# A hybrid attention, RWKV and mixture-of-experts layer: banks read at the chunk's end, the branch for crowded experts at expert 24, the end reordered

## The chip, the core and the metric

The kernel runs on one core of a Trainium2 chip. The metric is the time of one execution on the device in microseconds; lower is better. The core has TensorE (PE in the profile; PEld is its weight load), VectorE (DVE), ScalarE (ACT), GpSimd (POOL) and SyncE (SP), each with its own instruction stream that runs in order; a q behind a name is the engine's sequencer. TensorE writes to eight PSUM banks of 512 fp32 values per partition; the other engines read them out.

## The reference, cut to what matters

The input is 256 tokens of width 1024, in fp32. With weights of the usual kind:

```python
proj = x @ w_in                                   # 1024 x 5408
sh = token_shift(proj[..., :1824], mu_shift)      # t + (prev - t) * mu
y_rwkv = rwkv7_time_mix(...)                      # a recurrence over 256 steps, 8 heads of 64
y_attn = moba_attention(heads(q), heads(k), heads(v))   # 256 tokens are one block: causal softmax with rope
mixed = sigmoid(gate_a) * (y_attn @ w_attn_br) + sigmoid(gate_r) * (y_rwkv @ w_rwkv_br)
h = layer_norm(ALPHA * x + mixed @ w_out, ln1_g, ln1_b)
# moe_ffn: 32 experts, each token goes to 4 of them
logits = h @ w_router + b_router
top_vals, top_idx = top_k(logits, 4); gates = softmax(top_vals)
hid = h[tok] @ w1[e] + b1[e]                      # 1024 x 2048 for each expert
y = clamped_swiglu(hid) @ w2[e] + b2[e]           # 1024 x 1024 for each expert
acc[tok] += y * gate
out = layer_norm(ALPHA * h + acc, ln2_g, ln2_b)
```

Each expert is computed for 64 slots (CAP). Where an expert gets more than 64 tokens, extra rounds are needed; with these inputs no expert does, and the branch round that code is taken past it.

## The kernel before, in words

**Projections.** x @ w_in is done in 20 chunks of 256 columns. To keep fp32 accuracy each factor is split into a high and a low part (ACT at L128, DVE at L129), and each product is three matmuls (`mm3`, L135 to L137). A chunk is written into one bank, as two halves (h or tt) of eight steps (kt) each; chunks alternate between banks 0 and 1. Each step is a unit: a generator yields after it, and `fill(n)` puts n units of projection between other work on TensorE, so that TensorE has something to do while VectorE and ScalarE work on the recurrence, the softmax and so on. TensorE's order is the program's order (`manual_schedule`); the other engines' orders are made by the planner, within the program's data dependencies. These count a PSUM bank as a whole: an instruction of TensorE that writes into a bank waits for an earlier-written instruction that reads it, also where the two touch different halves.

The chunks' results are read out in three ways. `proj_shift` (L215) calls `shift`: a scaled copy on ScalarE (L205) and a multiply-add on VectorE (L206). `proj_tok` (L226) calls `done`: a copy on ScalarE (L258) for v, and rope on VectorE (L271 to L276) for q and k. `proj_gate` (L237) is a sigmoid on ScalarE (L245). In all three the read of a half stands behind the half's last unit (kt == 7). At L622 to L627 the rotated q and k are transposed in four groups through banks 6 and 7, and copied out by ScalarE.

**Experts.** Weights come in pairs of tiles, 2 MB each: four pairs for w1 and two for w2, for each of 32 experts. SyncE issues their loads (L733; for the last expert's w2 in nine pieces, L726). Ten pairs of buffers form a ring: `mdone` (L741) is called behind the last product that uses a pair and gives the pair to the next load; names put into `late` take a freed pair out of the ring for another use. A load also waits until the load eight before it has landed, as the eight DMA lanes (semaphores) are used in turn. For each expert TensorE does `first(e, 0)`, `first(e, 1)` (L1044) and `second(e)` (L1027), where `second` of an expert lies beside the next expert's `first`; `rows_out` (L1016, L1017) reads the result out, and `scatter` (L1009) adds it to the sums in banks 0 to 3.

**The end.** Behind the loop over experts stands the branch: each engine loads the largest token count (L1129) and jumps past the body for crowded experts, if there is none (the profile puts the jump and the semaphore steps behind it at L1206). The body uses four pairs that are free by then. Then come the second half of the last products: `second(30)`, the last expert's w2 in two halves of columns (L1221), each followed by its read-out, its scatter and its statistics (L1227), and the second norm (L1231 to L1250), whose last operations are split between VectorE, ScalarE and GpSimd.

## Time and profile before

| | us |
|---|---|
| median of 3 runs | 1246.01 (1243.99 to 1248.87) |
| the profiled execution | 1243.01, span 1241.2 |
| TensorE busy | 1133.4 (91%) |
| VectorE busy | 387.4 (31%) |
| ScalarE busy | 285.6 (23%) |
| DMA | 441.02 MB, mean 355 GB/s |

Busy shares are means over stages with different limits, so they say little here. The slices of the page cut the span into 40 parts of 31 us; the waits list what each engine waited for, with the total, the number and the longest; the timeline shows instructions in order of time, with the idle time in front of one and what ended it in square brackets.

### The profile page before, as it was taken

To read this page: it belongs to the slowest core of one execution; us is meant where nothing else is said; L and a number is where in the kernel's file an instruction comes from. 1 tells how busy PE (TensorE), PEld (TensorE's weight loads), DVE (VectorE), ACT (ScalarE), POOL (GpSimd) and SP (SyncE) were. 2 spreads that over 40 slices of the span, in tenths; PEclk is the share of its full clock that TensorE was granted. 3 is DMA by queue.
4 is the path that set the end of the run, shared out by engine and by line. 5 is a ranking of instruction groups with operands and counts; after the bars stand their busy time and mean duration, and the time that the engine had idled before them with its cause. 6 is when DMAs were issued, how large, how long until landed. Compare 5 with 4: busy or idle time off the path is not lost.

```text
span 1241.2 us, 15213 instructions
## 1 busy us (share of the span) xinstructions
PE 1133.4 (91%) x6434; PEld 596.0 (48%) x6434; DVE 387.4 (31%) x809; ACT 285.6 (23%) x577; POOL 6.5 (1%) x16
## 2 busy tenths in 40 slices
PE   8889887799999999999998989898999999999976
PEld 6678776798444343444433333343343333334322
DVE  4778466465222221222222121211121112222113
ACT  5534325444111111111111111111111111121112
POOL 0000000000000000000000000000000000000000
PEclk9999988899899999999999999999999999999997
DMA  7335423399699999999999999999999999999992
GB/s 269 106 116 156 150 94 145 135 364 380 264 429 427 428 427 429 427 427 418 426 426 430 426 427 429 428 426 428 427 428 427 429 427 428 427 427 427 428 414 87
DMA packets 45549, 441.02 MB, mean 355 GB/s; under 512 B 13010, under 2 KB 13538, under 8 KB 17954
## 3 DMA queue, kind: packets, MB, share of 16 engines
q1 hardware_dynamic: 36002, 436.93, 84.8%
q10 hardware_dynamic: 9472, 3.05, 1.1%
q8 instruction: 52, 0.85, 0.3%
q14 instruction: 23, 0.19, 0.0%
HBM read 438.13 MB, written 1.84 MB: 354 GB/s over the span
## 4 chain that ended last, share of the span: by engine, by line
DMA 49%; PE 41%; DVE 5%; ACT 4%; issue 1%; ACTq 0%; SPq 0%; DVEq 0%
DMA both<-in_w_dram 31%; DMA q<-in_w_dram 16%; PE b L1044 13%; PE b L1027 7%; PE b L135 4%; PE b L137 3%; PE b L136 3%; PE b L914 2%; DVE q L129 1%; PE b L1040 1%; ACT q L128 1%; DMA both<-in_win_dram 1%; PE b L1009 1%; PE b L1064 1%; ACT both L654 1%
## 5 line engine op out<-in xcount | busy, mean ns | idle before, releaser
L1044 PE MATMUL b<-both,s 128*64 128x512 f32 x1280 | 289.8, 600 | 20.4 <-DMA both<-in_w_dram 20.3
L1044 PEld LDWEIGHTS b<-both,s 128*64 128x64 f32 x1280 | 87.8, 138 | 204.7 <-issue 163.2
L1044 PE MATMUL b<-q,s 128*64 128x512 f32 x752 | 171.3, 601 | 4.0 <-DMA q<-in_w_dram 3.8
L1053 DVE TENSOR_SCALAR s<-b 128x256 f32<-128x256 f32 x64 | 27.2, 425 | 440.7 <-PE b L1044 440.7
L1027 PE MATMUL b<-both,s 128*64 128x512 f32 x576 | 128.9, 595 | 3.4 <-DMA both<-in_w_dram 3.4
L135 PE MATMUL b<-q,q 128*128 128x256 f32 x320 | 99.4, 311 | 33.4 <-ACT both L245 15.3
L1027 PE MATMUL b<-q,s 128*64 128x512 f32 x416 | 96.7, 612 | 8.5 <-DMA both<-in_w2l_dram 7.4
L1044 PEld LDWEIGHTS b<-q,s 128*64 128x64 f32 x752 | 51.2, 138 | 107.8 <-issue 97.6
L1069 ACT COPY s<-b 128x256 f32<-128x256 f32 x64 | 23.7, 371 | 323.0 <-PE b L1064 241.1
L137 PE MATMUL b<-q,q 128*128 128x256 f32 x320 | 93.5, 292 | 0.8 <-DVE q L129 0.8
L136 PE MATMUL b<-q,q 128*128 128x256 f32 x320 | 93.5, 292 | 0.0
L1017 DVE TENSOR_TENSOR s<-b,s 64x512 fp32r<-64x512 f32 (+1 forms) x66 | 44.4, 673 | 129.2 <-ACT s L1016 126.8
L135 PEld LDWEIGHTS b<-q,q 128*128 128x128 f32 x320 | 64.3, 201 | 41.0 <-ACT both L245 16.7
L1016 ACT CAST s<-b 64x512 fp32r<-64x512 f32 (+1 forms) x66 | 37.5, 568 | 191.2 <-PE b L1027 178.6
L1027 PEld LDWEIGHTS b<-both,s 128*64 128x64 f32 x576 | 40.4, 137 | 79.5 <-issue 77.8
L914 PEld LDWEIGHTS b<-s,s 128*128 128x128 f32 x512 | 61.7, 200 | 13.8 <-issue 13.0
L914 PE MATMUL b<-s,s 128*128 128x128 f32 x512 | 65.0, 287 | 1.4 <-DVE rt L958 0.7
L137 PEld LDWEIGHTS b<-q,q 128*128 128x128 f32 x320 | 64.3, 201 | 1.0 <-DVE q L129 1.0
L136 PEld LDWEIGHTS b<-q,q 128*128 128x128 f32 x320 | 64.7, 202 | 0.2 <-issue 0.2
L1054 ACT ACTIVATE s<-s 128x256 f32<-128x256 f32 x64 | 27.0, 421 | 143.8 <-DVE s L1053 143.8
L1027 PEld LDWEIGHTS b<-q,s 128*64 128x64 f32 x416 | 29.6, 140 | 62.4 <-issue 59.9
L129 DVE TENSOR_TENSOR q<-both,q 128x1024 fp32r<-128x1024 f32 x44 | 52.5, 1218 | 16.9 <-ACT q L128 16.6
(294 smaller groups left out, 1078.2 us busy)
## 6 DMA issues: line engine op xcount, KB each, us to landing
both<-in_w_dram SPq DMA_DIRECT2D x116, 2048.0 KB, 39.1
q<-in_w_dram SPq DMA_DIRECT2D x73, 2048.0 KB, 39.1
both<-in_win_dram SPq DMA_DIRECT2D x19, 1024.0 KB, 5.1
both<-in_wout_dram SPq DMA_DIRECT2D x4, 1024.0 KB, 7.2
both<-in_w2l_dram SPq DMA_DIRECT2D x7, 512.0 KB, 25.9
s<-in_wbr_dram SPq DMA_DIRECT2D x2, 1024.0 KB, 6.2
both<-in_wbr_dram SPq DMA_DIRECT2D x2, 1024.0 KB, 4.9
s<-in_w_dram SPq DMA_DIRECT2D x2, 1024.0 KB, 16.0
```

Source lines behind the costliest of these rows:

```text
L129: V.tensor_tensor(hl[:, 1, c], RAW[n][:, c], hl[:, 0, c].bitcast(FT), op=OP.subtract)
L135: PE.matmul(ps, lhs[0], rhs[0], start=first, stop=False)
L136: PE.matmul(ps, lhs[0], rhs[1], start=False, stop=False)
L137: PE.matmul(ps, lhs[1], rhs[0], start=False, stop=last)
L914: PE.matmul(pg[d // 4][:, d % 4], xtok[:, tt, 128 * d:128 * d + 128], oh[:, tt], start=tt == 0 and d % 4 == 0, stop=tt == 1 and d % 4 == 3)
L1016: A.copy(hi, ps)
L1017: V.tensor_tensor(lo, ps, hi.bitcast(FT), op=OP.subtract)
L1027: PE.matmul(ps[64 * n:64 * n + 64], aTs[e % 2][:, b, hf, 64 * g_:64 * g_ + 64], w[:, hf, 512 * n:512 * n + 512], start=ft == 0, stop=ft == 7)
L1044: PE.matmul(ps[64 * g_:64 * g_ + 64], XG[:, kt, 64 * j:64 * j + 64], w[:, kt % 2, 512 * g_:512 * g_ + 512], start=False, stop=kt == 7)
L1053: V.tensor_scalar(gl, pv[:, :, 0], 7.0, None, op0=OP.min)
L1054: A.activation(sw, gl, AF.Sigmoid, scale=1.702)
L1069: A.copy(aTs[e % 2][:, b], ps[:, 2 * i:2 * i + 2])
```

## The change

1. In the three projection helpers both halves of a bank are read out behind the chunk's last unit (h + kt == 8, that is h = 1 and kt = 7); the gate's two sigmoids become one over the whole bank.
2. The transposes of q and k go through banks 6, 7, 2 and 3.
3. The register load and the branch, with their body, stand at the start of expert 24 (MORE). The body's four pairs are the first four that come free from expert 21 on; they don't go back to the ring. The body itself is the same but for one small tile's place.
4. Behind the loop, the first scatter and its statistics stand between the two halves of the last expert's second product, in place of behind its first.
5. The second norm does three of its four quarters on VectorE, each as two operations with a PSUM bank between them, and the fourth on ScalarE and GpSimd; before, the third was on ScalarE and VectorE.

```diff
@@ -219,8 +219,10 @@
             for kt in range(8):
                 mm3(ps[:, h], [HL[n][:, x, kt, 128 * h:128 * h + 128] for x in range(2)], (xh[:, kt], xl[:, kt]),
                     kt == 0, kt == 7)
-                if kt == 7:
-                    shift(dst[:, f0 + h], ps[:, h], mc + h)
+                if h + kt == 8:
+
+                    for hh in range(2):
+                        shift(dst[:, f0 + hh], ps[:, hh], mc + hh)
                 yield
 
     def proj_tok(n, b, done):
@@ -230,8 +232,9 @@
             tk = slice(128 * tt, 128 * tt + 128)
             for kt in range(8):
                 mm3(ps[:, tt], (xh[:, kt, tk], xl[:, kt, tk]), [HL[n][:, x, kt] for x in range(2)], kt == 0, kt == 7)
-                if kt == 7:
-                    done(tt, ps[:, tt])
+                if tt + kt == 8:
+                    for t2 in range(2):
+                        done(t2, ps[:, t2])
                 yield
 
     def proj_gate(n, b, dst):
@@ -241,8 +244,8 @@
             for kt in range(8):
                 mm3(ps[:, h], [HL[n][:, x, kt, 128 * h:128 * h + 128] for x in range(2)], (xh[:, kt], xl[:, kt]),
                     kt == 0, kt == 7)
-                if kt == 7:
-                    A.activation(dst[:, h], ps[:, h], AF.Sigmoid)
+                if h + kt == 8:
+                    A.activation(dst, ps, AF.Sigmoid)
                 yield
 
     def units():
@@ -620,7 +623,7 @@
     qk = G_["qk"]
     qkT = slot(20, [2, 4, T])
     for f in range(4):
-        ps = bank(6 + f % 2, (2, T))
+        ps = bank((6, 7, 2, 3)[f], (2, T))
         for w in range(2):
             for tt in range(2):
                 PE.transpose(ps[:, w, 128 * tt:128 * tt + 128], qk[:, w, tt, 128 * f:128 * f + 128], ident)
@@ -1002,6 +1005,8 @@
 
     REST = (12, 14, 16, 18, 20)
 
+    MORE = 24
+
     def scatter(p, ns=(0, 1)):
         for n in ns:
             for tt in range(2):
@@ -1078,8 +1083,105 @@
                       start=True, stop=True)
         A.copy(ln2[:, i // 2, 512 * (i % 2):512 * (i % 2) + 512], ps.rearrange("p m n -> p (m n)"))
 
+    def overflow():
+
+        most = nc.values_load(cnt_i[0:1, 0:1], min_val=0, max_val=T)
+
+        spare = [v for u in range(4) for t in (pair(LATE["more", u]),) for v in (t[:, 0], t[:, 1])]
+        w = [v.rearrange("p (k n) -> p k n", k=2) for v in spare[:4]]
+        b1t, o4 = spare[4].rearrange("p (a b n) -> p a b n", a=2, b=2), spare[5].rearrange("p (a n) -> p a n", a=4)
+        sw4, sml = spare[6].rearrange("p (a n) -> p a n", a=8), spare[7]
+        xg = sml[:, 1280:1792].rearrange("p (d s) -> p d s", d=8)
+        ohf, ysb = sml[:, 0:256].rearrange("p (t x s) -> p t x s", t=2, x=2), sml[:, 256:768]
+        aT = sml[:, 768:1280].rearrange("p (b h s) -> p b h s", b=2, h=2)
+        pb = {i: bank(i) for i in (4, 5, 6, 7)}
...
+
+        with tc.If(most > CAP):
+            rot = rt[:, 0:2, :, 0:E]
+            V.tensor_scalar(rot[:, 0], posm, -float(CAP), None, op0=OP.add)
+            V.tensor_copy(rot[:, 1], gate)
+            for b in range(1, T // CAP):
+                with tc.If(most > CAP * b):
+                    with tc.For_i(0, E, 1) as e:
+                        more(e, rot)
+        return spare
+
     for e in range(E):
         p, j = divmod(e, 2)
+        if e == MORE - 3:
+            late.update({("more", u): 1 for u in range(4)})
+        if e == MORE:
+            order.__exit__(None, None, None)
+            spare = overflow()
+            order = tc.manual_schedule(engines={mybir.EngineType.PE})
+            order.__enter__()
         quarter = divmod(REST.index(e), 2) if e in REST[:4] else None
         if quarter:
             residual(*quarter)
@@ -1124,107 +1226,33 @@
         if E - 5 <= e < E - 1:
             second_norm_rows(e - E + 5)
     A.activation(lst[:, 0, 15:16], sw[:, 0:1], AF.Sqrt)
+    second(E - 2, lambda: turn(E - 1, (1,)))
+
+    def last_rows(n, fts):
+        for ft in fts:
+            b, g_, hf = ft // 4, (ft // 2) % 2, ft % 2
+            for a in range(2):
+                PE.matmul(py_[n][a][64 * a:64 * a + 64, 0:256], aTs[1][:, b, hf, 64 * g_:64 * g_ + 64],
+                          MW[E - 1, 8 + 2 * n + ft // 4][:, ft % 4, 256 * a:256 * a + 256], start=ft == 0, stop=ft == 7)
+
+    def last_out(n):
+        for a in range(2):
+            rows_out(E - 1, 512 * n + 256 * a, py_[n][a][64 * a:64 * a + 64, 0:256])
+
+    def last_scatter(n):
+        scatter(E // 2 - 1, (n,))
+        for tt in range(2):
+            V.bn_stats(out=lst[:, tt, 6 * n:6 * n + 6], in_=acc[2 * tt + n])
+
+    py_ = [[bank(4 + 2 * n + a) for a in range(2)] for n in range(2)]
+    last_rows(0, range(8))
+    last_out(0)
+    last_rows(1, range(4))
+    last_scatter(0)
+    last_rows(1, range(4, 8))
+    last_out(1)
+    last_scatter(1)
     order.__exit__(None, None, None)
-
-    most = nc.values_load(cnt_i[0:1, 0:1], min_val=0, max_val=T)
-
...
-    with tc.If(most > CAP):
-        rot = rt[:, 0:2, :, 0:E]
-        V.tensor_scalar(rot[:, 0], posm, -float(CAP), None, op0=OP.add)
-        V.tensor_copy(rot[:, 1], gate)
-        for b in range(1, T // CAP):
-            with tc.If(most > CAP * b):
-                with tc.For_i(0, E, 1) as e:
-                    more(e, rot)
-    with tc.manual_schedule(engines={mybir.EngineType.PE}):
-        second(E - 2, lambda: turn(E - 1, (1,)))
-        for n in range(2):
-            ps = [bank(4 + 2 * n + a) for a in range(2)]
-            for ft in range(8):
-                b, g_, hf = ft // 4, (ft // 2) % 2, ft % 2
-                for a in range(2):
-                    PE.matmul(ps[a][64 * a:64 * a + 64, 0:256], aTs[1][:, b, hf, 64 * g_:64 * g_ + 64],
-                              MW[E - 1, 8 + 2 * n + ft // 4][:, ft % 4, 256 * a:256 * a + 256], start=ft == 0, stop=ft == 7)
-            for a in range(2):
-                rows_out(E - 1, 512 * n + 256 * a, ps[a][64 * a:64 * a + 64, 0:256])
-            scatter(E // 2 - 1, (n,))
-            for tt in range(2):
-                V.bn_stats(out=lst[:, tt, 6 * n:6 * n + 6], in_=acc[2 * tt + n])
 
     zs = spare[0].rearrange("p (t n) -> p t n", t=2)
     ov = out_d[0].rearrange("(t p) n -> p t n", p=128)
@@ -1236,18 +1264,28 @@
         A.activation(st[:, 14:15], st[:, 13:14], AF.Sqrt, bias=eps[:, 1:2])
         V.reciprocal(st[:, 14:15], st[:, 14:15])
     A.activation(st[:, 15:16], st[:, 15:16], AF.Copy, scale=st[:, 14:15])
-    for tt in range(2):
-        zt, st = zs[:, tt], lst[:, tt]
-        for n in (1, 0) if tt else (0, 1):
-            c = slice(512 * n, 512 * n + 512)
-            if tt:
-                A.activation(zt[:, c], acc[2 * tt + n], AF.Identity, scale=st[:, 14:15], bias=st[:, 15:16])
-                for x, op in enumerate((OP.mult, OP.add)):
-                    (G if n else V).tensor_tensor(zt[:, c], zt[:, c], ln2[:, x, c], op=op)
-            else:
-                V.scalar_tensor_tensor(zt[:, c], acc[2 * tt + n], st[:, 12:13], ln2[:, 0, c], op0=OP.subtract, op1=OP.mult)
-                V.scalar_tensor_tensor(zt[:, c], zt[:, c], st[:, 14:15], ln2[:, 1, c], op0=OP.mult, op1=OP.add)
-            (nc.scalar if n and tt else nc.sync).dma_start(ov[:, tt, c], zt[:, c])
+    zp = {(0, 0): bank(4), (0, 1): bank(5), (1, 0): bank(6)}
+
+    def centred(tt, n):
+        V.scalar_tensor_tensor(zp[tt, n], acc[2 * tt + n], lst[:, tt, 12:13], ln2[:, 0, 512 * n:512 * n + 512],
+                               op0=OP.subtract, op1=OP.mult)
+
+    def scaled(tt, n):
+        c = slice(512 * n, 512 * n + 512)
+        V.scalar_tensor_tensor(zs[:, tt, c], zp[tt, n], lst[:, tt, 14:15], ln2[:, 1, c], op0=OP.mult, op1=OP.add)
+        nc.sync.dma_start(ov[:, tt, c], zs[:, tt, c])
+
+    c = slice(512, 1024)
+    A.activation(zs[:, 1, c], acc[3], AF.Identity, scale=st[:, 14:15], bias=st[:, 15:16])
+    for x, op in enumerate((OP.mult, OP.add)):
+        G.tensor_tensor(zs[:, 1, c], zs[:, 1, c], ln2[:, x, c], op=op)
+    nc.scalar.dma_start(ov[:, 1, c], zs[:, 1, c])
+    centred(0, 0)
+    centred(0, 1)
+    scaled(0, 0)
+    scaled(0, 1)
+    centred(1, 0)
+    scaled(1, 0)
 
 
 _ORDER = [(512, 1024), (0, 512), (1024, 1536), (1824, 5408)]
```

## Rows read from the trace of the kernel before

**Rows 1.** The page's slices: GB/s that the DMA engines moved, in 40 slices.
```profile
GB/s 269 106 116 156 150 94 145 135 364 380 264 429 427 428 427 429 427 427 418 426 426 430 426 427 429 428 426 428 427 428 427 429 427 428 427 427 427 428 414 87
```
**Rows 2.** Stages: length, busy PE, PEld, DVE, ACT, POOL, PE clock, DMA share, GB/s.
```profile
220.00:240.00 20.00, 13.90 (x87) 13.00 (x87) 8.95 (x12) 10.00 (x24) 0.00 (x0) 0.80 0.36 142
900.00:1200.00 300.00, 279.18 (x1402) 112.42 (x1400) 58.91 (x137) 45.86 (x111) 0.00 (x0) 0.99 1.01 427
```
**Rows 3.** TensorE's waits, 0 to 325 us: total, times, longest.
```profile
PE b L135 <- ACT both L245: 15.3, 7, 6.1
PE b L135 <- DVE both L274: 7.8, 4, 3.2
PE b L135 <- DVE both L206: 5.4, 3, 2.2
PE b L135 <- DVE s L206: 3.6, 2, 2.5
PE b L577 <- DVE both L571: 2.8, 1, 2.8
...
PE b L626 <- ACT both L627: 1.1, 1, 1.1
...
PE b L465 <- DVE s L206: 0.9, 1, 0.9
```
**Rows 4.** The timeline of TensorE: start, duration, instruction, idle time before it.
```profile
118.46 0.38 PE L135 MATMUL b<-q,q 128*128 128x256 f32 x1 [0.47 <-ACT both L245]
124.94 0.38 PE L135 MATMUL b<-q,q 128*128 128x256 f32 x1 [0.47 <-ACT both L245]
...
217.05 0.58 PE L135 MATMUL b<-q,q 128*128 128x256 f32 x1 [6.09 <-ACT both L245]
...
233.92 0.58 PE L135 MATMUL b<-q,q 128*128 128x256 f32 x1 [6.10 <-ACT both L245]
```
**Rows 5.** The timeline of ScalarE, before the first of the two long waits ends.
```profile
215.32 1.28 ACT L245 ACT_TABLE_LOAD   x1
```
**Rows 6.** Line L1206 by engine: duration in ns (min/median/max), first and last start.
```profile
L1206 SPq EVENT_SEMAPHORE  x8: 17/17/17, 1217.7 to 1218.8; - x8
...
L1206 PEldq COMPARE_BRANCH  x1: 6226/6226/6226, 1197.7 to 1197.7; - x1
...
L1206 DVEq COMPARE_BRANCH  x1: 76/76/76, 1202.7 to 1202.7; - x1
...
L1206 DVEq EVENT_SEMAPHORE  x1: 21/21/21, 1208.3 to 1208.3; - x1
```
**Rows 7.** The page's DMA issues: times, KB each, us to landing.
```profile
both<-in_w_dram SPq DMA_DIRECT2D x116, 2048.0 KB, 39.1
...
out_dram<-both SPq DMA_DIRECT2D x3, 256.0 KB, 2.0
```
**Rows 8.** The chain that ended last, 1130 us on: start, length, what.
```profile
1162.76 40.83 DMA q<-in_w_dram
```
**Rows 9.** The timeline of TensorE behind 1200 us.
```profile
1208.43 6.57 PE L1027 MATMUL b<-q,s 128*64 128x512 f32 x16 [7.38 <-DMA both<-in_w2l_dram]
...
1218.78 3.62 PE L1221 MATMUL b<-both,s 128*64 128x256 f32 x32
...
1224.65 3.67 PE L1221 MATMUL b<-both,s 128*64 128x256 f32 x32
1229.16 1.48 PE L1009 MATMUL b<-s,OT 128*128 128x512 f32 x4 [0.84 <-ACT s L1016]
```
**Rows 10.** The timeline of VectorE and GpSimd in the second norm.
```profile
1232.65 0.75 DVE L1249 SCALAR_TENSOR_TENSOR both<-both,lst,both 128x512 f32<-128x512 f32 x1
...
1233.95 2.93 POOL L1246 TENSOR_TENSOR both<-both,both 128x512 f32<-128x512 f32 x2 [1154.70 <-ACT both L1244]
...
1234.09 1.67 DVE L1249 SCALAR_TENSOR_TENSOR both<-both,lst,both 128x512 f32<-128x512 f32 x1
1235.68 2.47 DVE L1246 TENSOR_TENSOR both<-both,both 128x512 f32<-128x512 f32 x2
```

135 lines of the change are left out of this document (64 added, 71 removed).

## The prediction, made before the changed kernel ran

> **What bounds the kernel now.** I read the page's slices first, then the stage table, TensorE's waits, and the last 45 us instruction by instruction. The slices show two regimes: up to the ninth slice the DMA rate goes up and down, and from the twelfth on it stands at 414 to 430 GB/s without a break until the last but one [rows 1]. The stage table says the same of 900 to 1200 us: 427 GB/s, DMA share 1.01, TensorE busy 279.18 of 300 us [rows 2]. So the experts are bound by their weights (one load is 2.097 MB, at 427 GB/s 4.91 us; an expert has six, 29.5 us), and TensorE has 20.8 us in 10.2 experts to spare, 2.0 us each. The part before, some 320 us with TensorE busy most of the time, sets when that stream can run; the part behind the last landing is a chain. A microsecond saved in front moves the whole stream, because each weight load is released by work in front that frees its buffer. A microsecond saved on TensorE inside the stream is worth nothing.
>
> **In front: the waits in the middle of a chunk.** TensorE's waits before 325 us put 15.3 + 7.8 + 5.4 + 3.6 = 32.1 us on one instruction, L135, the first product of a unit, released by L245 (the sigmoid), L274 (the rotation) and L206 (the shift) [rows 3]. All three are readers of a projection's bank. That the waits stand in the middle of a chunk is seen in their spacing: two of them are 124.94 - 118.46 = 6.48 us apart, the length of one chunk of 48 products and its wait [rows 4]: there is one per chunk, and both rows are first products of the chunk's ninth unit. So the second half's first product waits until the first half has been read out of the same bank. The change emits both reads behind the last product. The next user of that bank is two chunks on (banks 0 and 1 alternate), so each read has a whole chunk, some 6.5 us, to finish in. The 32.1 us go as they stand; what counts is what is late next.
>
> - L245, 15.3 us in seven waits: two of them take 6.09 and 6.10 us [rows 4]. There ScalarE sits in the softmax exponentials and has to load a table (1.28 us) before the sigmoid [rows 5]. The next that needs ScalarE's result is the transpose of the scores some 30 units on; at 6.48 / 16 = 0.4 us a unit that is 12 us, and ScalarE's backlog is at most the 6 us that are waited for now. I keep 14 of 15.3; the sigmoid of chunk 18 may still hold up chunk 20 for 1 to 2.
> - L274, 7.8 us in four: these are VectorE behind its queue. The longest (3.2) stands where the recurrence has not begun, and goes. The others lie in the recurrence, where VectorE is also in the chain: L577 already waits 2.8 us for L571 [rows 3], and two rotations at once, 1.3 us each, stand in that queue. I keep 5.5.
> - L206, 9.0 us in five: consumers follow soon. The transposes of v at L465 already wait 0.9 us for a shift [rows 3]; two shifts at the end cost about 0.4 us more on each of ScalarE and VectorE at each of five such places. I keep 7.
> - Four banks in place of two for the transposes of q and k: L626 waits 1.1 us for L627's copy [rows 3]; 1.0 goes.
> - The clock: behind the two 6 us waits the same product takes 0.58 us where it takes 0.38 after a short one [rows 4], and the granted clock of 220 to 240 us is 0.80 [rows 2], so it had fallen to its lower level (1.2 of 2.4 GHz) after TensorE stood still. Without these waits I estimate 2.5 us back.
> - One 512-wide sigmoid in place of two 256-wide ones is ScalarE time that nobody waits for: 0.
>
> Sum in front: 14 + 5.5 + 7 + 1 + 2.5 = 30 us. The bounds: 32.1 + 1.1 + 3.5 = 37 above; below, all waits that VectorE released come back at the consumers (16.8 lost), both later reads cost 0.8 us at five places (4), and the clock gives nothing, which leaves about 12. I take 30, as most rows name a backlog that has a chunk's time to drain.
>
> **The branch at expert 24.** The rows of L1206 show what skipping the branch costs each engine [rows 6]. TensorE's branch instruction takes 6226 ns; VectorE's own takes 76 ns, but its next one comes 5.5 us later (1202.7 to 1208.3). SyncE then has eight semaphore steps, the last at 1218.8: it raises the count of each of the eight DMA lanes, and each only after that lane's last transfer. No engine waits for all others, but SyncE can issue nothing until every load before the branch has landed.
>
> Moved to expert 24, this empties the load queue once. Up to the branch SyncE has issued all six pairs of expert 24's stretch, since four of the ten pairs are held back from expert 21 for the branch's body. The last of the six is issued when TensorE ends second(22), about 5 pairs or 25 us before it lands. During these 25 us the DMA engines work; then they stand until SyncE's next issue comes through. A 256 KB store lands 2.0 us after its issue [rows 7], of which 0.6 is transfer at 427 GB/s, so with the issue (0.33) and the lane steps some 2 us are lost, and up to 4 when the 16 engines don't end together. I take 3; below there is no gain, above 8 if the instruction that follows has to be fetched first.
>
> TensorE loses more, but not on the path. Its stall here is that of the end now, 7.38 us, and behind it 16 products take 6.57 us where 32 of half the width take 3.62 [rows 9], so 2.9 us of lower clock: some 10 to 12 us. The stream falls back by 3 at the same place, so 7 to 9 us have to be caught up at 2.0 an expert: done by expert 28 or 29 of 31. This works only if the loads are still released in time. With six pairs a load is needed 6 x 4.91 = 29 us after the one before it in its buffer; using it up takes 3.6 [rows 9], the lag 12, the issue 1.7, other products in between up to 8: it holds with 4 us to spare. The loads' 39.1 us from issue to landing [rows 7], eight times 4.9, are only the queue's depth, and nothing is lost when it becomes 20. SyncE's own branch and register load lie inside the drain.
>
> **The end.** The last loads of the stream land at 1203.6 (first half of expert 30's second product [rows 8]), 1208.5 and, 4 MB later, at about 1218.3; SyncE's lane steps end there too [rows 6]. Now TensorE stands at the branch until 1208.43, then runs at the lower clock [rows 9]. Without it: first half 1203.6 to 1207.25; second 1208.5 to 1212.15; last product's first half 3.62, to 1215.8; half of its second half, 1.8, to 1217.6 (its piece has landed); the first scatter, which now needs no wait as the 0.84 us read-out [rows 9] lies beside those products, to 1218.8; the rest, 1.8, to 1220.6. The same point is now 1224.65 + 3.67 = 1228.3. Gain 7.7; if the clock falls in the 2.9 us pause before 1203.6, 1.8 less.
>
> The second norm: VectorE now ends 1235.68 + 2.47 = 1238.15, and one of its scalings takes 1.67 us beside GpSimd where the same one before took 0.75 [rows 10]. New are six operations, all through PSUM; the first scaling starts at 1232.65 now, and with it five of 0.75 us are left at most, so VectorE is done at about 1236.4. Then GpSimd's 2.93 us are the last, to 1236.9, in place of 1238.15; both are followed by a store of 2.0 us [rows 7]. About 1.1 us gained. By the Trainium skill, SBUF — State Buffer, section Who interferes with whom, a VectorE instruction with two SBUF inputs contends with a GpSimd one that reads SBUF, and one with at most one does not; by that rule the new scalings, with one input in PSUM, take 0.75. Were the slow one slow for another reason, two of them would take 1.67 and the 1.1 us would be gone. The trace agrees as far as it goes: 1.67 is 0.75 and the rest of GpSimd's first operation. The end together: 7.7 + 1.1, about 9 us (5.5 to 10).
>
> **Sum.** 1243.0 (the profiled execution, span 1241.2) - 30 - 9 + 3 = 1207. The median of the runs shown, 1246.0, is 3.0 above that execution, so I expect a median of 1210.
>
> **Rivals.**
> - *The waits only move.* VectorE and ScalarE are in the chains in front; half of the 30 comes back at L379, L465, L577 and the transposes. For it: VectorE releases 16.8 of the 32.1 us [rows 3]. Against it: ScalarE's 15.3 have slack behind them. 1210 + 15 = 1225.
> - *No gain in front.* The second half goes on waiting, or the wait goes to the next chunk's start because both reads end late: only the end and the branch count, 1246 - 9 + 3 = 1240. Against it: the banks alternate, and a read of less than 1 us has a chunk of 6 us to end in.
> - *Slower: the small ring starves the stream.* Place: experts 24 to 31, six pairs. If TensorE's lag passes some 16 us, a load is issued only when the queue is empty, and each of 48 pairs costs its 1.7 us of issue again: 82 us, 1246 - 39 + 82 = 1289. It decides from the 4 us above. By the Trainium skill, Runtime: NRT & Kernel Launch, section Instruction fetch mechanics, a taken branch out of the prefetched pages stalls for a fetch; that rule speaks for a stall at expert 24 on each engine, and the rows of L1206 show it on two. The lag is worked out from those rows and stays below the point; and SyncE's drain gives TensorE 25 us of landed weights.
>
> **How the numbers follow.** Forecast 0.72, waits move 0.18, no gain in front 0.05, ring starves 0.03, others 0.02. The forecast's own range is 1202 to 1222 (front 24 to 36, end 5.5 to 10, branch 2 to 6); the waits-move case reaches to 1231. So 1200 to 1231 holds 8 in 10. Half a per cent (6 us) is what can be told from no change: faster 0.94, same 0.03, slower 0.03.
>
> **What would show it.** Right: L135 no longer waits for L245, L274 or L206; the first expert product comes some 30 us earlier; the DMA rate has one dip of 2 to 4 us after expert 24's loads and TensorE one pause of 7 to 10 us about 25 us before it; TensorE waits for landings again before expert 30; no pause of TensorE over 3 us at the end. Wrong: a new wait of several us at L379, L465, L577 or L664; gaps in the DMA rate in experts 25 to 31; the stream's last landing earlier by much less than 27 us.

## The result: 1202 us in place of 1247, and the profile after

| | before | after |
|---|---|---|
| median, us | 1247.4 (1244.0 to 1249.2, 4 runs) | 1202.2 (1197.9 to 1203.5, 4 runs) |
| ratio, 95% interval | | 0.963 [0.960, 0.967] |
| span of the profiled execution, us | 1241.2 | 1200.3 |
| first bias product of expert 0 (L1040, now L1045), at us | 317.0 | 282.4 |
| the same of expert 24 | 975.1 | 948.7 |
| the same of expert 31 | 1184.3 | 1154.2 |
| from expert 0's first product to the end, us | 924.2 | 917.9 |

The forecast was 1210, the range 1200 to 1231. Read by place: 34.6 us were gained ahead of the experts. TensorE's lead (how much earlier it starts the same product than in the kernel before) is 34.8 us at expert 23, 26.4 at expert 24 and 30.1 from expert 27 on, 4.7 less than ahead of the branch. It ends at 40.9, so 10.8 come behind expert 31's first product.

The slices of the page after (GB/s, 40 of 30 us) answer to [rows 1]: saturation begins in the eleventh slice, and the branch shows as one slice at 344.

```profile
GB/s 278 127 137 135 152 206 137 324 382 279 428 428 427 428 427 428 427 426 422 426 428 428 428 428 428 428 427 428 427 428 428 420 344 428 427 427 428 428 428 239
```

TensorE's waits after, 0 to 290 us, answer to [rows 3] (L558, L580, L426, L468 and L382 were L555, L577, L423, L465 and L379). Every wait of L135 for a reader of its bank is gone (what is left at L135 is a wait for its input, L128); three waits of 2 to 3.4 us in the recurrence lead now.

```profile
PE b L558 <- DVE both L552: 3.4, 1, 3.4
PE b L580 <- DVE both L574: 3.1, 1, 3.1
PE b L426 <- DVE s L410: 2.2, 1, 2.2
PE b L468 <- DVE s L206: 1.6, 1, 1.6
...
PE b L135 <- ACT q L128: 0.9, 1, 0.9
```

The stage ahead of expert 0, TensorE alone: length, busy time (products), granted clock, DMA share, GB/s; of the kernel before, and then after.

```profile
0.00:316.99 316.99, 271.69 (x2089) 0.93 0.55 194
```
```profile
0.00:282.37 282.37, 262.30 (x2088) 0.95 0.60 218
```

Length less busy time is standing still: 45.3 before, 20.1 after, so 25.2 us of waits went. The other 9.4 are the same products in less busy time, at a higher clock (0.95 for 0.93). The clock accounts for most of them: 0.07 of 317 us is 22 us of full clock not granted, 0.05 of 282 is 14.

Line L1166 after, by engine, answers to [rows 6].

```profile
L1166 SPq EVENT_SEMAPHORE  x8: 17/17/17, 946.4 to 966.3; - x8
...
L1166 PEldq COMPARE_BRANCH  x1: 5912/5912/5912, 936.3 to 936.3; - x1
...
L1166 DVEq COMPARE_BRANCH  x1: 76/76/76, 942.8 to 942.8; - x1
L1166 DVEq EVENT_SEMAPHORE  x1: 21/21/21, 948.6 to 948.6; - x1
```

The rate while SyncE takes those steps (windows, columns as above):

```profile
958.00:960.00 2.00, 2.00 (x12) 1.00 0.87 369
960.00:962.00 2.00, 2.00 (x12) 1.00 0.71 303
962.00:964.00 2.00, 2.00 (x12) 1.00 0.53 221
964.00:966.00 2.00, 2.00 (x12) 1.00 0.08 33
966.00:968.00 2.00, 2.00 (x24) 1.00 0.42 82
968.00:970.00 2.00, 2.00 (x11) 1.00 0.68 229
```

Against 427 GB/s the six fall short by 58, 124, 206, 394, 345 and 198; times 2 us and over 427, that is 6.2 us of transfer not done. The busy share falls step by step over 8 us, from 0.98 at 956 to 0.08. It is a mean over 16 engines, so I read the steps as one engine after the other having nothing left; these views don't show the engines singly. TensorE's pause is in this trace too, and its last products (timeline) answer to [rows 9]: no pause above 0.91 us is left.

```profile
948.74 1.19 PE L1045 MATMUL b<-b1r,pick 128*128 128x512 f32 x2 [8.20 <-DVEq L1166]
...
1171.80 3.65 PE L1032 MATMUL b<-q,s 128*64 128x512 f32 x16 [0.87 <-DMA q<-in_w_dram]
...
1176.72 3.65 PE L1032 MATMUL b<-both,s 128*64 128x512 f32 x16 [0.91 <-DMA both<-in_w_dram]
1180.21 5.35 PE L1235 MATMUL b<-both,s 128*64 128x256 f32 x48
...
1189.39 1.48 PE L1014 MATMUL b<-s,OT 128*128 128x512 f32 x4 [0.84 <-ACT s L1021]
```

The second norm on VectorE, and its GpSimd part, answer to [rows 10]. Of the two scalings in the first row, the first is nearly over when GpSimd starts at 1194.18; the second runs beside it, and so do the last two operations on VectorE. Each takes 0.74 to 0.75 us.

```profile
1193.52 1.40 DVE L1275 SCALAR_TENSOR_TENSOR both<-b,lst,both 128x512 f32<-128x512 f32 x2
...
1195.63 0.75 DVE L1275 SCALAR_TENSOR_TENSOR both<-b,lst,both 128x512 f32<-128x512 f32 x1
```
```profile
1194.18 2.61 POOL L1281 TENSOR_TENSOR both<-both,both 128x512 f32<-128x512 f32 x2 [1119.62 <-ACT both L1279]
```

### The profile page after: what moved, and what is told of

It is laid out like the page before. It is cut to its first block, busy times and chain, and to the rows that moved or that the text cites. A ratio compares the mean times of both kernels' runs of the same rounds, so it can differ in the third digit from the quotient of the medians.

```text
span 1200.3 us, 15200 instructions
## 1 busy us (share of the span) xinstructions
PE 1124.0 (94%) x6434; PEld 590.3 (49%) x6434; DVE 384.2 (32%) x809; ACT 280.1 (23%) x566; POOL 6.1 (1%) x16
## 5 line engine op out<-in xcount | busy, mean ns | idle before, releaser
L1049 PE MATMUL b<-both,s 128*64 128x512 f32 x1456 | 331.9, 605 | 17.5 <-DMA both<-in_w_dram 17.4
L1049 PEld LDWEIGHTS b<-both,s 128*64 128x64 f32 x1456 | 100.8, 139 | 227.8 <-issue 190.7
L1032 PE MATMUL b<-both,s 128*64 128x512 f32 x624 | 139.7, 595 | 4.0 <-DMA both<-in_w_dram 3.2
L1049 PE MATMUL b<-q,s 128*64 128x512 f32 x576 | 132.4, 606 | 1.6 <-DMA q<-in_w_dram 1.5
L135 PE MATMUL b<-q,q 128*128 128x256 f32 x320 | 96.6, 302 | 0.9 <-ACT q L128 0.9
L137 PE MATMUL b<-q,q 128*128 128x256 f32 x320 | 92.9, 290 | 0.8 <-DVE q L129 0.8
L136 PE MATMUL b<-q,q 128*128 128x256 f32 x320 | 92.8, 290 | 0.0
L1032 PEld LDWEIGHTS b<-both,s 128*64 128x64 f32 x624 | 43.8, 137 | 86.5 <-issue 82.7
L1032 PE MATMUL b<-q,s 128*64 128x512 f32 x368 | 83.0, 597 | 0.9 <-DMA q<-in_w_dram 0.9
L1021 ACT CAST s<-b 64x512 fp32r<-64x512 f32 (+1 forms) x66 | 37.4, 567 | 189.5 <-PE b L1032 177.8
L1049 PEld LDWEIGHTS b<-q,s 128*64 128x64 f32 x576 | 39.7, 139 | 81.6 <-issue 76.7
L135 PEld LDWEIGHTS b<-q,q 128*128 128x128 f32 x320 | 63.6, 199 | 5.2 <-issue 2.6
L129 DVE TENSOR_TENSOR q<-both,q 128x1024 fp32r<-128x1024 f32 x44 | 52.4, 1218 | 10.6 <-ACT q L128 10.6
L1045 PE MATMUL b<-b1r,pick 128*128 128x512 f32 x128 | 47.2, 451 | 8.2 <-DVEq L1166 8.2
```

Source lines behind the costliest of these rows:

```text
L129: V.tensor_tensor(hl[:, 1, c], RAW[n][:, c], hl[:, 0, c].bitcast(FT), op=OP.subtract)
L135: PE.matmul(ps, lhs[0], rhs[0], start=first, stop=False)
L136: PE.matmul(ps, lhs[0], rhs[1], start=False, stop=False)
L137: PE.matmul(ps, lhs[1], rhs[0], start=False, stop=last)
L1021: A.copy(hi, ps)
L1032: PE.matmul(ps[64 * n:64 * n + 64], aTs[e % 2][:, b, hf, 64 * g_:64 * g_ + 64], w[:, hf, 512 * n:512 * n + 512], start=ft == 0, stop=ft == 7)
```

## Experiments

All ratios are to the kernel before, run beside them on the same chip. "Front" is where expert 0's first product starts in the profiled execution, "rest" the span from there to the end. Rest repeats within 2 us for the same code (922.3 to 924.3 in the five profiles with end and branch as before, 917.9 and 917.3 in the changed kernel's two); front only within about 5 (see the last group).

| run | median, us | ratio, interval | front | rest |
|---|---|---|---|---|
| gate_only | 1215.1 | 0.974 [0.971, 0.978] | 294.5 | 922.9 |
| tok_shift | 1230.3 | 0.987 [0.984, 0.990] | 307.3 | 922.3 |
| front_all | 1207.6 | 0.969 [0.966, 0.973] | 278.0 | 924.1 |
| keep_warm | 1241.1 | 0.996 [0.995, 0.998] | 312.1 | 924.3 |
| branch_end | 1204.5 | 0.966 [0.963, 0.970] | 281.2 | 920.7 |
| no_branch | 1195.7 | 0.961 [0.959, 0.963] | 278.6 | 915.3 |
| short_body | 1196.8 | 0.961 [0.959, 0.963] | 282.2 | 914.6 |
| act_loads | 1200.5 | 0.964 [0.962, 0.966] | 279.7 | 917.2 |
| old_end | 1205.2 | 0.967 [0.966, 0.969] | 283.1 | 920.1 |
| after_again | 1199.9 | 0.963 [0.961, 0.966] | 278.6 | 917.3 |
| pool_body | 1196.6 | 0.960 [0.957, 0.962] | 282.0 | 914.7 |
| warm_route | 1196.1 | 0.960 [0.957, 0.963] | 275.8 | 915.0 |

### The front, edit by edit

gate_only, on the kernel before:

```diff
-                if kt == 7:
-                    A.activation(dst[:, h], ps[:, h], AF.Sigmoid)
+                if h + kt == 8:
+                    A.activation(dst, ps, AF.Sigmoid)
```

tok_shift has the late read in `proj_shift` and `proj_tok` instead; front_all has all three late reads and the four banks.

> The kernel before with one edit: the gate's sigmoid reads its bank once, behind the chunk's last unit. My theory: ScalarE's backlog has a chunk's time to drain, so 14 of the 15.3 us that L135 waited for L245 go, and the clock gives 2.5 us back: 16 to 17 us shorter, ratio about 0.987, the first expert product 16 us earlier than before, and no wait of L135 for L245. Rival (the waits only move): half of it comes back at the next consumer of ScalarE's results, 7 to 8 us shorter, ratio about 0.994, with new TensorE waits for ScalarE of 7 us in sum.

> The kernel before with two edits: the token shift (L206) and the rotation and the copy of v (L274, L258) read both halves behind the chunk's last unit; the gate as before. My theory: 7 of 9.0 us at L206 and 5.5 of 7.8 us at L274 go: 12.5 us shorter, ratio 0.990. Rival (the waits only move, because VectorE is itself in the recurrence's chain): the 16.8 us come back at the consumers, 0 to 4 us shorter, ratio 0.997 to 1.000, and the waits for L245 stay 15 us or grow. If the edits add up, gate and these two together give the 34.6 us that the first expert product came earlier in the changed kernel; if one hides the other's gain, the sum of the two runs differs from 34.6 by more than 4.

> The kernel before with all edits in front (late reads of all three kinds, four banks for the transposes of q and k); branch and end as before. My theory: the first expert product comes 34.6 us earlier, as in the changed kernel, and the end comes 34 to 35 us earlier too, because the weight stream moves as a whole: ratio 0.972. Rival (the stream is bound by the DMA from the beginning of the kernel, and the gain in front is given back while the buffers are filled): the first expert product is early but the last landing is not, 20 us or less at the end, ratio 0.984 or more.

Measured: 30, 15 and 37 us shorter by the medians. The stages ahead of expert 0 (columns as above), gate_only, tok_shift, front_all:

```profile
0.00:294.52 294.52, 265.39 (x2088) 0.95 0.57 209
```
```profile
0.00:307.34 307.34, 270.36 (x2088) 0.93 0.56 200
```
```profile
0.00:278.00 278.00, 257.62 (x2088) 0.97 0.60 216
```

Standing still is 29.1, 37.0 and 20.4 us, so 16.2, 8.3 and 24.9 less than the 45.3 of before. The first two add up to the third (24.5): the waits are independent of each other, and gate's 16 confirm that ScalarE's backlog had a chunk's time to drain. (The late read and the merging of two sigmoids into one weren't tried apart.) The two longest waits of tok_shift that are no sigmoid show what VectorE's later reads gave back, the same as in the changed kernel:

```profile
PE b L557 <- DVE both L551: 3.4, 1, 3.4
PE b L579 <- DVE both L573: 3.1, 1, 3.1
```

So "the waits only move" is right for about half of VectorE's 16.8 us, and wrong for ScalarE's 15.3. Busy time is 6.3, 1.3 and 14.1 us less, and the clock says why. Full clock not granted in front, (1 - granted clock) x length, is 22 us before and 15, 22 and 8 in the three: gate_only gets 7 us back, tok_shift none, front_all 14. In gate_only the clock is 1.00 from 200 to 240 us, where the two long waits were. front_all has this too, and in the 20 us round the end of its front the clock stays at 1.00, where it is 0.73 and 0.76 in gate_only (280 to 300 us) and 0.84 and 0.65 in tok_shift (290 to 310). No edit touches that last stretch; the last group shows that it differs between executions.

By the medians the gate alone is worth nearly twice my 16 to 17, and gate and the rest together (44.5) are more than front_all's 37.4; by the fronts the two give 32.1, beside 34.6 in the changed kernel and 39.0 in front_all. With intervals of some 4 us on each of the three, and one profile of each, the runs don't settle whether that difference is real. The profiled execution of gate_only was the longest of its four and that of front_all the shortest, which is why their spans and medians disagree. The rival for front_all is out: the lead of 39.0 at expert 0 is 39.2 at expert 31.

### The clock by itself

keep_warm, on the kernel before (no result of these products is read):

```diff
+                if n in (18, 19) and h and not kt:
+                    dm = bank(5, (2, T))
+                    for _ in range(44):
+                        PE.matmul(dm[:, 0], HL[n][:, 0, 0, 128:256], xh[:, 0], start=True, stop=True)
```

> The kernel before with one addition: 44 products whose result nobody reads stand ahead of TensorE's two waits of 6.1 us for the sigmoid (44 x 0.12 us = 5.3 us, so the wait is filled and not shortened). My theory: the two waits cost more than their length, since TensorE runs at the lower clock for some 3.5 us behind each; with TensorE kept busy, the clock of 210 to 240 us stays at 1.0 and the first expert product comes 3 us earlier than in the kernel before (16 products of 0.21 us become 0.12 us, twice). Rival (the clock has nothing to do with these waits): the clock falls as before and the first expert product comes no earlier, or later by what the products exceed the wait.

Measured: 4.9 us shorter by the medians, though 44 products were added twice and both waits end as late as ScalarE lets them. The windows of 220 to 240 us and the first products behind the two waits, to be read against [rows 2, 4]:

```profile
220.00:240.00 20.00, 19.16 (x152) 1.00 0.41 158
```
```profile
218.53 0.38 PE L135 MATMUL b<-q,q 128*128 128x256 f32 x1 [0.82 <-ACT both L249]
...
233.65 0.39 PE L135 MATMUL b<-q,q 128*128 128x256 f32 x1 [0.84 <-ACT both L249]
```

The clock is 1.00 where it was 0.80, the product takes 0.38 us where it took 0.58. Followed product by product, keep_warm is 1.5 us late ahead of the two waits (its 1380th product starts at 196.0, before at 194.6) and 2.2 early behind them (the 1580th at 236.3 and 238.5): 3.7 us of clock from these two waits alone. The rest of the lead of 4.9 at expert 0 comes later, in the routing phase (the choice of experts and the gathering of their tokens), which this edit doesn't touch.

### The branch: at the end, gone, and with a short body

branch_end, on the changed kernel, with the hooks in the loop removed (no pair is withheld) and the body's four pairs taken from the free list:

```diff
+    order.__exit__(None, None, None)
+    spare = overflow()
+    order = tc.manual_schedule(engines={mybir.EngineType.PE})
+    order.__enter__()
     second(E - 2, lambda: turn(E - 1, (1,)))
```

no_branch removes the call of `overflow` at expert 24, and four pairs are withheld as before; short_body keeps the branch:

```diff
-            for b in range(1, T // CAP):
-                with tc.If(most > CAP * b):
-                    with tc.For_i(0, E, 1) as e:
-                        more(e, rot)
+            PE.transpose(pb[7][:, 0:128], xtok[:, 0, 0:128], ident)
+            A.copy(sml[:, 0:128], pb[7][:, 0:128])
```

> The changed kernel with the branch and its body put back behind the loop over experts (ahead of the last two second products), with the ring of ten pairs kept whole; front, order of the last products and second norm as changed. My theory: the drain at expert 24 goes (4.7 us of the stream are kept) and the stall of TensorE at the end comes back (7.4 us, and 2.9 us of lower clock behind it, of which some 2.5 us are saved by the new order of the last products): 4 to 7 us longer than the changed kernel, 1206 to 1209 by the profile, ratio to the kernel before 0.967 to 0.970. Rival (the gain at the end is the order's and the norm's alone, the branch's place is worth nothing): 4 to 5 us shorter than the changed kernel, 1196 or less, ratio 0.960. Second rival (a small ring costs the stream something too): the last landing comes more than 4.7 us earlier than in the changed kernel.

> The changed kernel without the register load, the branch and the body for crowded experts (that part is left out); the four pairs are withheld from expert 21 all the same, so the ring has six. My theory: all of the 4.7 us that the stream lost at expert 24 is SyncE's drain, and a ring of six pairs costs nothing: 4 to 5 us shorter than the changed kernel, no dip of the DMA rate after expert 24's loads, first expert products of 24 to 31 all 34 to 35 us earlier than in the kernel before. Rival (the smaller ring costs part of it): some of the 4.7 us stays, gaps in the DMA rate in experts 24 to 31 without a branch.

> The changed kernel with the branch kept at expert 24 but a body of five short instructions with no transfer in it (the rounds for crowded experts are left out). My theory: SyncE has no lane counts to raise, so it doesn't wait for the landings: the drain goes, 4 to 5 us shorter than the changed kernel. TensorE's pause of 8.2 us and the 5.7 us until VectorE's next instruction stay if they are the price of any taken branch at this place, and shrink to below 2 us if they come from the distance of the jump (the code behind it is then within what was loaded already). The time is the same either way, as that pause is off the path. Rival: SyncE's wait belongs to the branch and not to the body's transfers: same time as the changed kernel, dip of the DMA rate as there.

branch_end: TensorE's stall is back, with the lower clock behind it:

```profile
1173.01 5.08 PE L1032 MATMUL b<-q,s 128*64 128x512 f32 x16 [7.75 <-DVEq L1166]
```

Its rest is 2.8 to 3.4 us longer than the changed kernel's, a little below the 4 to 7 that I expected; by the times alone, 0.966 [0.963, 0.970] beside 0.963, the two can't be told apart. no_branch and short_body agree on the drain: at expert 31 TensorE has gained 4.7 and 4.5 us (no_branch's lead over the changed kernel grows from 3.8 to 8.5), in the rest 2.0 to 3.3. The landings in the traces, counted from expert 0's first product, show where the 6.2 us go. The loads behind the branch land 3.1 to 3.5 us later in the changed kernel's two profiles than in no_branch, and soon 4.2 to 4.7, so that is what the stream loses. The last two whole pairs (the last expert's w2 follows them in pieces) land only 2.7 to 3.3 later, since in no_branch and short_body the second last comes 6.2 us behind the one before it, where 4.9 are usual. Why it is late there stays open. The table cuts the rest at the last whole pair's landing, which is counted from expert 0's first product:

| | last whole pair lands, us | from there to the end of the last scatter | from there to the end of the span |
|---|---|---|---|
| before | 891.4 | 22.3 | 10.6 |
| after | 894.3 | 14.2 | 9.4 |
| after_again (below) | 893.8 | 14.2 | 9.4 |
| branch_end | 890.8 | 20.5 | 9.4 |
| no_branch | 891.0 | 14.9 | 9.3 |
| short_body | 891.0 | 14.2 | 9.4 |
| pool_body (below) | 891.0 | 14.2 | 9.5 |
| old_end (below) | 894.2 | 15.4 | 10.6 |

So the branch costs 6.3 us at the end (20.5 for 14.2), and the drain at expert 24 costs 2.7 to 3.3 there. In no_branch and short_body TensorE waits 2.2 us for expert 30's second product, where it waits 0.87 in the changed kernel; in no_branch its clock falls there, and the 16 products behind take 5.35 us for 3.65, which gives 0.7 back. The rate is 428 GB/s from 900 to 1150 us in no_branch, with six pairs:

```profile
900.00:1150.00 250.00, 229.67 (x1148) 0.99 1.01 428
```

So a ring of six pairs costs nothing. And short_body says what TensorE's pause is (TensorE reaches the branch there 11 us later, as the order of its work changed). Its line L1166, by engine:

```profile
L1166 PEldq COMPARE_BRANCH  x1: 236/236/236, 947.3 to 947.3; - x1
...
L1166 DVEq COMPARE_BRANCH  x1: 76/76/76, 951.7 to 951.7; - x1
L1166 DVEq EVENT_SEMAPHORE  x1: 21/21/21, 952.0 to 952.0; - x1
```

TensorE's jump takes 236 ns where it took 5912, VectorE's next instruction comes 0.3 us after its jump where it took 5.8, and there is no row for steps of SyncE at all. In these runs the pause comes with a long body, the drain with transfers in the body. By the Trainium skill, Runtime: NRT & Kernel Launch, section Instruction fetch mechanics, a taken branch whose target lies outside the code already fetched waits for a fetch; these two runs agree with it, 236 ns beside 5912, though no row shows the fetch itself.

### Who issues across the drain

act_loads: the first four loads behind the branch come from ScalarE.

```diff
+            q = nc.scalar if handover else nc.sync
...
-            nc.sync.dma_start(t.rearrange("p a b -> p (a b)"), src)
+            q.dma_start(t.rearrange("p a b -> p (a b)"), src)
```

> The changed kernel with the first four weight loads behind the branch issued by ScalarE in place of SyncE. ScalarE passes the branch in 0.5 us and does not wait for landings, and TensorE frees these pairs at about 955, 958, 962 and 966 us, before SyncE's drain ends at 966.3. My theory: the DMA engines have work through the drain, the dip of the DMA rate goes, and the end comes 3 to 4.7 us earlier than in the changed kernel, ratio to the kernel before 0.960. Rival (a load that ScalarE issues also waits for the lane's earlier load, or holds up ScalarE's sigmoids, so TensorE is late): the same time as the changed kernel or up to 5 us longer.

My theory fell. The timeline of ScalarE shows the first of these loads at 963.29, right when SyncE's last step (963.2) raises the count of the lane that the load uses, and a copy of ScalarE's own held up behind it; TensorE then waits for that copy for 3.9 us:

```profile
963.29 0.85 ACTq L739 DMA_DIRECT2D both<-in_w_dram  x2
964.18 0.37 ACT L1077 COPY s<-b 128x256 f32<-128x256 f32 x1 [16.70 <-SPq L1169]
```

The lanes are shared: a load that ScalarE issues, too, waits until the skipped body's share of its lane's count has been raised, and SyncE raises them one after the other (in the changed kernel at 951.64, 956.54, 961.42 and 966.28, each behind that lane's landing; the first load uses the lane that is raised last). So I moved the transfers in the body to other lanes. pool_body, on the changed kernel:

```diff
-                    nc.sync.dma_start(w[i], src.rearrange("o p (k n) -> p (o k) n", n=1024))
+                    nc.gpsimd.dma_start(w[i], src.rearrange("o p (k n) -> p (o k) n", n=1024))
...
-                nc.scalar.dma_start(b1t[64 * g_:64 * g_ + 64, 0, b],
+                nc.gpsimd.dma_start(b1t[64 * g_:64 * g_ + 64, 0, b],
```

> The changed kernel with the same branch at expert 24, but the transfers in its body (weights and bias rows for crowded experts) are issued by GpSimd in place of SyncE and ScalarE. My theory: what SyncE waits for behind the jump are the counts of the lanes that its own transfers in the body would have raised; with none of them there, SyncE issues on, the dip of the DMA rate goes, and the end comes 3 us earlier than in the changed kernel (as in the kernel without the body's transfers), ratio to the kernel before 0.960 to 0.962. TensorE's pause of 8 us stays, as the jump is as long as before, and costs nothing. Rival: the loads behind the branch wait for GpSimd's lanes as they waited when ScalarE issued them, no gain; second rival: the pause of 8 us then becomes what counts, 4 to 8 us longer.

Line L1166 by engine, and the 12 us in which the rate had fallen, in two windows:

```profile
L1166 POOLq EVENT_SEMAPHORE  x4: 17/43/43, 286.4 to 286.7; - x4
...
L1166 PEldq COMPARE_BRANCH  x1: 6072/6072/6072, 935.8 to 935.8; - x1
L1166 SPq COMPARE_BRANCH  x1: 50/50/50, 940.6 to 940.6; - x1
```
```profile
958.00:964.00 6.00, 6.00 (x30) 1.00 1.02 429
964.00:970.00 6.00, 6.00 (x42) 1.00 1.00 426
```

SyncE has no steps left; GpSimd passed the branch at 287 us, as it had nothing else to do. TensorE's pause stays (8.2 us) and its lag is made up by expert 27. The rest is 2.6 to 3.2 us shorter, and the last whole pair lands 2.7 to 3.3 earlier. Run side by side, the medians are 1196.6 and 1199.9; the intervals, [0.957, 0.962] and [0.961, 0.966], just overlap, so the rate and the landings carry the claim, not the times alone. This is the whole computation. No run takes the branch, so what the body costs when GpSimd issues its transfers isn't shown.

### The end's two parts

old_end puts the first scatter and its statistics back behind the first half of the last products, and restores the old second norm:

```diff
-    last_rows(0, range(8))
-    last_out(0)
-    last_rows(1, range(4))
-    last_scatter(0)
-    last_rows(1, range(4, 8))
-    last_out(1)
-    last_scatter(1)
+    for n in range(2):
+        last_rows(n, range(8))
+        last_out(n)
+        last_scatter(n)
```

> The changed kernel with the old order of the last products (first scatter and statistics behind the first half, then the second half) and the old second norm; branch at expert 24 and front as changed. My theory: the order is worth the read-out that TensorE waits for (0.84 us twice, one of them saved) and the half of the products that had to wait for the scatter, about 1.5 us together, and the norm 1.1: 2 to 3 us longer than the changed kernel. Rival (the 10.8 us at the end are mostly order and norm, not the branch's stall): 5 us longer or more. Second rival (the norm's new operations gain nothing, as VectorE's scalings are slow beside GpSimd): 1.5 us longer or less.

The rest is 2.2 to 2.8 us longer. From the end of the last scatter to the end of the span it is 1203.2 - 1192.7 = 10.5 us, with the new norm 1200.3 - 1190.9 = 9.4: the norm is worth the predicted 1.1. The order is worth 1.1 to 1.7 by the rest, 1.2 by the table above (15.4 for 14.2). In old_end VectorE's scaling beside GpSimd takes 1.67 us again, and the two operations behind it, which the new norm no longer has, 2.47:

```profile
1196.12 1.67 DVE L1274 SCALAR_TENSOR_TENSOR both<-both,lst,both 128x512 f32<-128x512 f32 x1
1197.71 2.47 DVE L1271 TENSOR_TENSOR both<-both,both 128x512 f32<-128x512 f32 x2
```

### Why the front differs between executions

after_again is the changed kernel unaltered. warm_route is pool_body with nine products on TensorE that nobody reads, in the four short waits of the routing phase:

```diff
+    def busy(n):
+        for _ in range(n):
+            PE.transpose(bz[:, 0], cA[:, 0:128], ident)
...
+        if n >= len(todo):
+            busy(2)
...
+    busy(2)
     gather_rows(pg, 0)
...
+    busy(3)
     gather_rows(pg, 1)
```

> The changed kernel once more, beside the three others of this call, as what they are compared with: 1198 to 1204 us. My theory on the spread between executions: the clock falls in the routing phase just ahead of the experts (270 to 285 us) in some executions and not in others, behind the same waits of 0.5 to 0.75 us, and moves the first expert product by 4 us (278 or 282 us).

> As the run with GpSimd's transfers, and in addition nine products on TensorE whose result nobody reads, 2 or 3 of them in each of the four waits of 0.5 to 0.75 us in the routing phase. My theory: the clock falls there because TensorE stands still for short times, so with less of it the first expert product comes at 278 us in every execution: 2 to 4 us shorter than the run without them by the median, and the executions lie closer together. Rival (the fall has another cause than these waits): the same time, or 1 us longer for the products.

Nine profiles share the changed front as it is; it is 278.0 to 283.1 us long in them. In the timeline the same 16 products of the gather, behind the same wait, take 3.78 us in the changed kernel's first profile and 2.05 in front_all's:

```profile
273.36 3.78 PE L917 MATMUL b<-s,s 128*128 128x128 f32 x16 [0.61 <-DVE rt L876]
```
```profile
272.68 2.05 PE L916 MATMUL b<-s,s 128*128 128x128 f32 x16 [0.61 <-DVE rt L875]
```

The windows of 270 to 280 us (columns as above), in the changed kernel and in front_all:

```profile
270.00:280.00 10.00, 8.04 (x39) 0.59 1.03 437
```
```profile
270.00:280.00 10.00, 8.12 (x60) 1.00 1.04 441
```

They show the granted clock at 0.57 to 0.66 in seven of the nine, and at 1.00 in front_all, no_branch and, with the added products, warm_route. From the gather's first product to expert 0's it is 5.3 us in these three, and 7.4 to 9.2 in the seven.

So the fall costs 2 to 4 us, but my theory that it alone decides between 278 and 282 fell in its own run: after_again has the fall (0.66, 8.1 us) and a front of 278.6, as its gather starts at 270.5, where the others' starts at 271.6 to 274.8. What sorts the nine is the clock of the whole front: 0.97 in the two shortest (278.0 and 278.6), 0.96 in the next two (278.6 and 279.7), 0.95 in the five of 281.2 to 283.1. The same products take 257.6 and 257.7 us of busy time at 0.97 and 261.6 to 263.9 at 0.95. Why the clock of the same code differs between executions stays open.

In warm_route the front is the earliest of all (275.8, clock 0.98), but its median is that of pool_body (1196.1 and 1196.6, ratios 0.9599 and 0.9597): the prediction of 2 to 4 us is not borne out by the times. The added products don't hold the clock up in every execution: over the whole run it is 0.980 and 0.981 in the two shortest of the five (1192.5 and 1193.0 us), but 0.973 and 0.974 in the other three (1196.1 to 1200.0), no more than pool_body's 0.971 to 0.977. Where it fell in those three isn't shown.

## Why the prediction was right, and where its terms were off

- **What bounds it.** Right. A lead in front moves the whole stream: 39.0 us at expert 0 are 39.2 at expert 31 in front_all, and its rest of 924.1 us is that of before. The rest, where end and branch were to give -9 + 3 = -6, fell by 6.3 and 6.9 us in the changed kernel's two profiles.
- **Front, the waits.** Predicted 14 + 5.5 + 7 + 1 = 27.5 us; 25.2 in the profile, near enough. The gate gave 16.2, its own 15.3 and a little behind them, the shift and the rotation 8.3 in place of 12.5: here the cover was thinner than I took it, as VectorE is in the recurrence's chain. Of the four wrong signs that I named, the waits at L577 and L465 (now L580 and L468) are there, 3.1 and 1.6 us, though only 0.3 and 0.7 longer than before; the larger new ones are at L558 and L426, which I hadn't named.
- **Front, the clock.** The mis-sized term: 2.5 us predicted, 3.5 as its upper bound. The two long waits alone cost 3.7 (keep_warm), and the same products took 9.4 us less busy time in the changed kernel, 14.1 in front_all. I priced only the products right behind two waits, and left out the other stretches of low clock; the front came out 34 to 39 us shorter in place of 30, and front_all's 39.0 is past the 37 that I had as the most.
- **The branch.** Place and mechanism right: one pause of TensorE of 8.2 us (7 to 10 predicted), then a dip of the rate, 18 us after the pause begins (some 25 predicted), TensorE's lag caught up (by expert 26, sooner than 28 or 29), and no starving afterwards. The size was too small: 6.2 us of transfer, 4.2 to 4.7 by the landings, where I took 3 and 4 at most unless a fetch came on top. I had counted the restart, and too little for the engines' unequal ends. That the last whole pair then lands 2.9 us later than before (894.3 and 891.4), my 3, is luck: 1.4 of the 4.7 come back at the last two pairs, for no reason that I had named.
- **The end.** 7.7 + 1.1 predicted. By the table, the last scatter ends 14.2 us behind the last whole pair where it was 22.3, so 8.1, and the norm gave 1.1; with the 2.9 this makes the 6.3 by which the rest fell. The norm's 1.1 is in part luck: its last operation ends 1.6 us sooner behind the last scatter (5.9 for 7.5), more than my 1238.15 - 1236.9 = 1.25, and the store behind it, ScalarE's now, gives some of that back. By the Trainium skill, SBUF — State Buffer, section Who interferes with whom, a VectorE instruction with at most one input in SBUF does not contend with GpSimd, outside its 2-port modes; the trace is in keep with it where the inputs moved to PSUM (0.74 to 0.75 us each for 1.67). My reading of the 1.67 was not exact: the rest of GpSimd's first operation (to 1235.21) and 0.75 would make 1.87.
- **The rivals.** "No gain in front" and "the small ring starves" are out (front_all, no_branch). "The waits only move" holds for about half of VectorE's share; the clock's larger return covered it, which was luck and not foresight.

In the profiled execution 1207 was forecast and 1202.0 came: 6.9 us more from the clock, 2.3 less from the waits, 0.3 more in the rest. The other 3 us up to 1210 are what I added because the median before lay above its profiled execution; after, the two are the same. 1202 lies at the lower edge of the range, and the median of after_again, 1199.9, just outside it.

## What to carry to other kernels

A bank that is read half by half costs a wait in the middle of each chunk, and where that wait is long it also costs the clock behind it: price both, and read the second from busy time of the same products, not from the waits. Before a skipped branch is put into a saturated stream, look which queues own transfers in its body; here the engine that owned them had to see its earlier transfers land, and ScalarE's loads waited with it, so the body's transfers went to an idle engine. Compare a stage by its own length (front, rest): the total hides that one repeats within 2 us and the other only within 5.

## What the runs showed of the hardware that was not expected

- A skipped body costs by what it contains: 0.3 us on VectorE and 236 ns on TensorE when it is a few instructions long, 5.8 us and 5.9 us when it is long. The DMA engines were moving weights at the full rate meanwhile in both (428 GB/s from 940 to 970 us in short_body).
- SyncE shows the same: its first step comes 5.2 us behind its jump in the changed kernel (941.2 to 946.4), though the lane that it raises had landed by 937.2; in pool_body, whose body holds no transfer of SyncE's, its next instruction comes 0.4 us behind the jump. The drain hides this.
- The DMA lanes' counts are common to SyncE and ScalarE: ahead of a load that ScalarE was to issue, it stood idle for 16.7 us, until SyncE's last step.
- The granted clock in the routing phase falls in some executions and not in others, behind the same waits of 0.5 to 0.75 us, and costs 2 to 4 us from the gather's first product to expert 0.
- Products that nobody reads, laid into two waits of 6 us, made the kernel before 4.9 us faster: 0.996 [0.995, 0.998].
